# The old value rows of a sliding-window cache: copied inside device memory instead of stored from on-chip tiles

## The chip, the core and the metric

The kernel runs on one core of a Trainium2 chip. The metric is the device time of one launch in microseconds; three runs of the kernel before gave 2320.72, 2321.75 and 2324.44 us, a median of 2321.75 us. TensorE (PE) does the matmuls, VectorE (DVE), ScalarE (ACT) and GpSimd (POOL) the rest, and every DMA of this program is issued by one engine, SyncE (SP), in program order. A DMA moves packets on up to 16 DMA engines of the core; one packet here is one contiguous run of bytes.

## The reference

One inference step of a decoder trunk with two layers: a prompt of 512 tokens and 8 samples of one new token each. Each layer is a half-step SwiGLU FFN, a token mixer, and a second half-step FFN. The mixer has a gated DeltaNet group and a sliding-window attention group. For the samples the attention reads a cache of the last 128 keys and values and returns the cache shifted by one token:

```
def _swa_step(q, k, v, k_buf, v_buf, sinks):
    kk = jnp.concatenate([k_buf, k], axis=1)      # 128 old rows, 1 new row
    vv = jnp.concatenate([v_buf, v], axis=1)
    ...                                           # softmax with a sink, o = p @ vv
    return o, kk[:, T:], vv[:, T:]                # T = 1: drops the oldest row
```

So rows 0 to 126 of the new value cache are rows 1 to 127 of the old one, unchanged, and row 127 is the new token's value. Eight samples, 127 rows of 128 float32 (2 heads of 64): 1016 rows of 512 bytes for each layer.

## The kernel before

All activations stay on chip with features on partitions. Weights are streamed: blocks of 512 KB go into three `raw` buffers, ACT rounds each half block to a float32r head (`whi`), DVE computes the rest (`wlo`), and PE multiplies in three passes. Eight split half blocks can be held. A load of `raw` waits until DVE has given out the `wlo` of the buffer's block before.

The order of all instructions is fixed when the program is built: `Fill` (L96) puts steps of the smaller computations between those of the big products, by an estimate of time (`Clock`, L40). On the chip each engine works in order, so an instruction that waits holds up all behind it on its engine.

The change touches the mixer, `mix` (L748). Its parts, as far as they are needed here:

- The input projection streams 22 tiles of `in_win`. Its small loads are issued first: `wraw`, then the rotary tables `cos` and `sin`, and after the first four tiles the convolution state (`misc<-in_convst`). In layer 0 this begins at about 455 us of the profile, in layer 1 at about 1597 us.
- `swa_sample` (L1330) is the attention of the samples. It loads the old keys into two tiles `kc` and the old values into two tiles `vc`, four samples each, with the cache row on the partition for `vc`. Later it stores the shifted keys (`out_ks<-kc`, L1359), the 127 old value rows of each half (`out_vs<-vc`, L1360), and last the new row (`out_vs<-vrow`). The tiles `vc` also feed the product with the softmax.
- The DeltaNet group builds for each head a matrix `B` on DVE. `dn_inverse` (L930) takes two heads at once: the diagonal blocks of 16 of `B` go out to device memory (`bs<-B`) and come back with another layout (`bb<-bs`); then a long chain of small DVE instructions (`t<-w,bb`, `w<-t`) builds the inverses.
- `swa_block` (L1249) is the attention of the prompt; its scores are the PE products `aux<-swa,swa`, and DVE reads them (`mx`) before PE may write the next ones.

In the program order of SP, the four stores of `swa_sample` and the new row stand directly ahead of `bs<-B`, `bb<-bs`, `bs<-B`, `bb<-bs` of the first two heads, and these ahead of the next three weight loads. Each DMA also uses one of eight completion semaphores in turn, so it waits for the DMA eight places before it to have landed.

Of the kernel before, what the change touches and what calls it, by code (L numbers as in the profile page):

```python
# [23 lines left out]
# Tiles of the input projection: q, k, v of the delta rule by head (c), k, v, q of attention (s), gates (z).  # L24
# [13 lines left out]
class Clock:  # L38
    """An estimate of when the engines are done with what they were given and when tiles are there,
    for the order of the trace."""  # L40
# [41 lines left out]
    def ring(self, tag, n, tile):  # L82
        """A new tile in a ring of n buffers: it is there when the one before it is given up."""
        r = self.rings.setdefault(tag, [])
        r.append(tile)
        if len(r) > n:
            k = self.key(r.pop(0))
            self.rd[self.key(tile)] = max(self.rd.get(k, 0.0), self.wr.get(k, (0.0,))[0])


class Fill:
    """Generators whose steps are put between those of the main products. A step is given to the
    engines when what it waits for should be there; those of a lower rank go first. A generator yields the
    tiles that its next step reads, a condition, or nothing: all that it has done so far."""
# [33 lines left out]
    def step(self):  # L128
        """One step that holds the tensor engine, with others that do not."""
        c = self.clk  # L130
        t = c.pe
        for n in range(TUNE["steps"]):
            e = None
            if all(c.free[q] <= c.pe + v for q, v in BACKLOG.items()):
                e = next((e for e in self.q if e[0] <= c.pe + 0.05 and (e[2] is None or e[2]())), None)
            if e is None:
                return n > 0
            self.run(e)
            if c.pe > t:
                break  # L140
        return True
# [17 lines left out]
class Stream:  # L159
    """Weight blocks in the order in which they are used: loads run ahead, and each half block  # L160
    (four k-tiles) is split into a float32r head and a float32r rest."""
# [10 lines left out]
    def add(self, ap, keep=None):  # L172
        """keep: takes the place of the rings; the split is held back until it says so."""
        self.descs.append(ap)
        n = ap.shape[1]
        for o in range(0, n, 512):
            self.subs.append((len(self.descs) - 1, o, min(512, n - o), o + 512 >= n, keep))

    def advance(self, done, must=-1):
        """Loads and splits as far as the buffers reach and the loads have come, and up to half block  # L180
        must; done: half blocks that are used up."""
        clk = self.ops.clk
        while True:
# [9 lines left out]
            j = len(self.todo)  # L193
# [19 lines left out]
    def rest(self):  # L213
        """The rest of a split is given out after the head of the next one."""
        if self.late:
            j, d, lo, raw, hi = self.late
            self.late = None
            self.ops.tt(out=lo, in0=raw, in1=hi, op=ALU.subtract)
            if d is not None:
                del self.raw[d]  # L220
                self.free_raw = d + 1
# [5 lines left out]
    def take(self, held=0):  # L227
        """The next half block; held: how many before it are still in use."""
        j = self.out
        self.advance(j - held, j)  # L230
        assert j < len(self.todo), (j, len(self.todo), held)
        if self.late and self.late[0] == j:
            self.rest()
            self.advance(j - held)
        self.out += 1
        return self.todo[j]


class Ops:
    """The engines' instructions, counted on the clock."""  # L240
# [96 lines left out]
def trunk(ctx, tc, xT, cT, cst, rope, vec, gu1, dn1, win, wba, wout, gu2, dn2, ada,  # L337
# [16 lines left out]
    # slots in use, and those promised to a part that takes them as it goes  # L354
# [17 lines left out]
    def hold(n):  # L372
        """Waits for n slots; they are given back with a negative number."""
        yield lambda: room_for(n)
        given[0] += n
# [23 lines left out]
    # ---------------------------------------------------------------- adaLN  # L399
# [8 lines left out]
    def ada_mm(t, pa, u=0, first=True, last=True):  # L408
        """m of 512 features, for all sequences, in rows 16 u + sequence: four k-tiles at once in columns
        of the array, summed over them when it is turned to features on partitions."""  # L410
        for k in range(KD):
            r = k % 4
            mm(pa[32 * r:32 * r + 32], lhsT=sc[:, u, k, :], rhs=t[k], start=first and k < 4, stop=last and k >= 4, frac=0.27)
# [6 lines left out]
    def ada_turn(l, g, m_sb, pt=None, n=1):  # L420
        """The n groups from g on to features on partitions, with what is added and multiplied."""
# [12 lines left out]
    def ada_gen(l0):  # L434
        """Works off what is left of adaLN up to layer l0, while there is room for its weights."""
# [29 lines left out]
    # ---------------------------------------------------------------- norm  # L465
    class Norm:
        """RMSNorm, shift and scale of x, half by half, split into head and rest."""
# [11 lines left out]
        def square(self, k, a, end=False):  # L479
            """x of tile k is there: its square joins the sum when the next one comes, or at the end."""  # L480
# [58 lines left out]
    # ---------------------------------------------------------------- products  # L539
    def mmk(out, w, k, src, kk, a, first, last, M=128):  # L540
        """One k-tile of a product in three passes: head by head, head by rest, rest by head."""
        wh, wl = w
        for wi, (wt_, part) in enumerate(((wh, 0), (wh, 1), (wl, 0))):
            mm(out, lhsT=wt_[:, k * M:(k + 1) * M], rhs=src(a, part, kk), start=first and wi == 0, stop=last and wi == 2)
# [11 lines left out]
    def product(src, nk=KD, k0=0, M=128):  # L556
        """One tile of a product, both halves; yields after each k-tile, then the banks."""
# [21 lines left out]
    def head(norm):  # L579
        """The first four tiles of a product, half by half, while the norm of x ends. The blocks  # L580
        hold two tiles by four k-tiles."""
# [24 lines left out]
    def first_head(norm, ada_late):  # L606
        """The head of the first product, by pairs of k-tiles as their shift and scale come, for as many
        of its tiles as there are banks."""
# [35 lines left out]
    def tail(l, j, items, nk, norm, src, last, wait=None):  # L644
        """The last tiles of a product, for one half of the tokens at a time; x and its norm follow.
        items: half, tile, whether its weights come now, whether they are used later, whether they
        are in the rings."""
# [35 lines left out]
    # ---------------------------------------------------------------- FFN  # L683
# [45 lines left out]
    # ---------------------------------------------------------------- mix  # L729
# [18 lines left out]
    def mix(l, norm):  # L748
# [23 lines left out]
        # ------------------------------------------------ gates  # L772
# [57 lines left out]
        # ------------------------------------------------ delta rule: before the scan  # L830
# [99 lines left out]
        def dn_inverse(pr):  # L930
            """Inverses of the blocks of 16 on the diagonal, of two heads."""
# [31 lines left out]
        def dn_merge(h):  # L963
            """Joined to blocks of 32, 64, 128."""
# [32 lines left out]
        # ------------------------------------------------ delta rule: the scan, two heads at a time  # L997
# [3 lines left out]
        def normed(o, zin, dst_hi, dst_lo, key):  # L1001
            """Gated RMSNorm of o (heads on the middle axis), split."""
# [77 lines left out]
        # ------------------------------------------------ delta rule: one step of the samples  # L1080
# [28 lines left out]
        def sample_pair(pr, qv, beg, d8, i8, bc, on):  # L1109
            """Rows 32 j + s of two heads: the products with the state, then what follows from them."""  # L1110
# [89 lines left out]
        # ------------------------------------------------ attention  # L1200
# [129 lines left out]
        def swa_sample():  # L1330
# [26 lines left out]
            for i in range(2):  # L1357
                ops.copy(out=kct[i][:, :, 128], in_=qn[:, 0, 4 * i:4 * i + 4])
                dma(out=ks_o[l, :, 4 * i:4 * i + 4, :], in_=kct[i][:, :, 1:129])  # L1359
                dma(out=vs_o[l, 4 * i:4 * i + 4, 0:127, :].rearrange("s k d -> k s d"), in_=vct[i][1:128])  # L1360
# [56 lines left out]
        # ------------------------------------------------ input projection  # L1417
        rope_t = [slot("cos", F32, (128, T)), slot("sin", F32, (128, T))]
        wraw = slot("wraw", F32, (128, KD, 32))
        dma(out=wraw, in_=wba[l])  # L1420
        dma(out=rope_t[0], in_=rope[:, 0])
# [40 lines left out]
        # b, a: between the others  # L1462
# [26 lines left out]
        # ------------------------------------------------ output projection  # L1489
# [24 lines left out]
    # ---------------------------------------------------------------- order of the weights  # L1514
# [27 lines left out]
    # ---------------------------------------------------------------- run  # L1542
    with tc.manual_schedule():
# [6 lines left out]
        def load(q, j):  # L1550
            """The weights for shift or scale of two k-tiles of x."""
# [105 lines left out]
def layout(i):  # L1657
    """The inputs as the chip takes them: blocks of weights with k on partitions, activations and
    states with features on partitions."""
# [26 lines left out]
    def head4(b):  # L1686
        """The first four tiles as blocks of two tiles by four k-tiles."""
# [77 lines left out]
```

## Time and profile before

| | |
|---|---|
| median of three runs | 2321.75 us (2320.72 to 2324.44) |
| span of the profiled execution | 2320.7 us; no other time is recorded for it |
| mean granted TensorE clock | 0.985 |
| PE busy | 2234.2 us, 96% of the span |
| DVE busy | 1084.8 us, 47% |
| ACT busy | 866.1 us, 37% |
| DMA queue of SP | 172708 packets, 285 MB, 38.4% of 16 engines |

The share of PE is an average: nearly all of the span it is the engine that sets the pace, with a few stretches in which it idles. Such stretches are where work on another engine, or a transfer, can move the end. The granted clock is given as a share of full speed, 2.4 GHz; 0.50 is the lower level of 1.2 GHz.

### The profile page before, as it was taken

The page shows a single profiled execution, that of the slowest core. Times are in us where ns is not written, and L with a number is a line of the kernel's source. Part 1 is how long each engine was busy: PE and PEld are TensorE (multiplying, and loading weights), DVE is VectorE, ACT ScalarE, POOL GpSimd, SP SyncE. Part 2 cuts the span into 40 slices and gives each one's busy share as a digit, 9 for nine tenths or more (in the row PEclk, how much of TensorE's full clock was granted, in tenths as well). Part 3 has the DMA queues.
Part 4 walks back from the last instruction along what each step waited for, and adds up shares of the span by engine and source line. Part 5 has one row for each costly group of instructions (what it writes and reads, how often), then busy time and mean ns, then how long its engine had stood idle before and what let it go on. Part 6 is the DMA issues. An engine that isn't in the chain of part 4 may idle for free.

```text
span 2320.7 us, 43783 instructions
## 1 busy us (share of the span) xinstructions
PE 2234.2 (96%) x18154; PEld 2122.6 (91%) x18154; DVE 1084.8 (47%) x2586; ACT 866.1 (37%) x1861; POOL 76.5 (3%) x73
## 2 busy tenths in 40 slices
PE   7999999999888999999999999999979889999999
PEld 5879999999777988999999999999878779999999
DVE  5323333565788733333344333335667777333332
ACT  4222332355645432233234333224637445333321
POOL 0000000000121000000000000000001200000000
PEclk8999999999899999999999999999989999999999
DMA  8994223343214589422323222324322243222331
GB/s 269 323 329 136 92 85 92 101 77 94 88 50 136 180 314 339 155 92 85 95 86 101 92 91 89 93 83 91 102 81 70 63 146 110 92 92 91 92 109 56
DMA packets 172907, 287.75 MB, mean 124 GB/s; under 512 B 49925, under 2 KB 87461, under 8 KB 172709
## 3 DMA queue, kind: packets, MB, share of 16 engines
q1 hardware_dynamic: 172708, 284.96, 38.4%
q8 instruction: 142, 2.33, 0.4%
q14 instruction: 57, 0.46, 0.1%
HBM read 270.51 MB, written 14.41 MB: 123 GB/s over the span
## 4 chain that ended last, share of the span: by engine, by line
PE 82%; DVE 7%; issue 5%; ACT 3%; DMA 2%; SPq 0%; POOL 0%; DVEq 0%; POOLq 0%
PE acc L263 67%; PE aux L263 15%; DVE wlo L298 1%; DVE s L298 1%; PE aux L273 1%; DMA bs<-B 1%; DVE t L298 1%; ACT sq L290 1%; DVE w L298 1%; DVE hl L298 0%; SPq L258 0%; DVE vr L298 0%; DMA bb<-bs 0%; DMA ada<-in_ada 0%; POOL swa L307 0%
## 5 line engine op out<-in xcount | busy, mean ns | idle before, releaser
L263 PE MATMUL acc<-hh,whi 128*128 128x256 f32 x3440 | 743.9, 290 | 26.9 <-DVE x L298 12.2
L263 PE MATMUL acc<-hh,wlo 128*128 128x256 f32 x3440 | 722.8, 285 | 1.2 <-DVE wlo L298 1.2
L263 PE MATMUL acc<-hl,whi 128*128 128x256 f32 x3440 | 722.9, 285 | 0.0
L290 ACT ACTIVATE whi<-raw 128x512 fp32r<-128x512 f32 (+1 forms) x672 | 406.2, 617 | 785.7 <-PE acc L263 619.7
L298 DVE TENSOR_TENSOR wlo<-raw,whi 128x512 fp32r<-128x512 f32 (+1 forms) x672 | 437.3, 681 | 377.4 <-ACT whi L290 376.9
L263 PEld LDWEIGHTS acc<-hh,whi 128*128 128x128 f32 x3440 | 549.1, 189 | 66.9 <-issue 33.3
L263 PEld LDWEIGHTS acc<-hh,wlo 128*128 128x128 f32 x3440 | 547.4, 189 | 2.5 <-DVE wlo L298 2.5
L263 PEld LDWEIGHTS acc<-hl,whi 128*128 128x128 f32 x3440 | 548.5, 190 | 0.2
L263 PE MATMUL acc<-ghi,whi 128*128 128x256 f32 x1232 | 262.2, 283 | 0.0
L263 PE MATMUL acc<-glo,whi 128*128 128x256 f32 x1232 | 262.2, 283 | 0.0
L263 PE MATMUL acc<-ghi,wlo 128*128 128x256 f32 x1232 | 262.1, 283 | 0.0
L298 DVE TENSOR_TENSOR g<-g,acc 128x256 f32<-128x256 f32 (+1 forms) x168 | 64.2, 422 | 342.5 <-PE acc L263 306.1
L263 PEld LDWEIGHTS acc<-glo,whi 128*128 128x128 f32 x1232 | 197.1, 189 | 0.0
L263 PEld LDWEIGHTS acc<-ghi,wlo 128*128 128x128 f32 x1232 | 196.9, 188 | 0.0
L263 PEld LDWEIGHTS acc<-ghi,whi 128*128 128x128 f32 x1232 | 196.7, 188 | 0.0
L290 ACT ACTIVATE ghi<-g 128x520 fp32r<-128x520 f32 x88 | 56.2, 639 | 219.5 <-DVE g L298 219.5
L298 DVE SCALAR_TENSOR_TENSOR x<-acc,mt,x 128x256 f32<-128x256 f32 x72 | 33.6, 481 | 141.9 <-PE acc L263 141.9
L298 DVE TENSOR_TENSOR glo<-g,ghi 128x520 fp32r<-128x520 f32 x88 | 61.7, 701 | 62.2 <-ACT ghi L290 62.2
L263 PE MATMUL aux<-hl,whi 128*128 128x264 f32 x304 | 86.8, 286 | 0.8 <-DVE hl L298 0.8
L263 PE MATMUL aux<-hh,whi 128*128 128x264 f32 x304 | 87.1, 286 | 0.0
L263 PE MATMUL aux<-hh,wlo 128*128 128x264 f32 x304 | 86.6, 285 | 0.0
L263 PE MATMUL aux<-ada,sc 128*32 128x512 f32 (+1 forms) x640 | 70.9, 571 | 6.7 <-DMA ada<-in_ada 6.7
(289 smaller groups left out, 2149.4 us busy)
## 6 DMA issues: line engine op xcount, KB each, us to landing
raw<-in_gu SPq DMA_DIRECT2D x176, 512.0 KB, 3.3
ada<-in_ada SPq DMA_DIRECT2D x288, 256.0 KB, 5.4
raw<-in_dn SPq DMA_DIRECT2D x64, 512.0 KB, 3.5
raw<-in_win SPq DMA_DIRECT2D x44, 512.0 KB, 3.3
raw<-in_dn SPq DMA_DIRECT2D x32, 384.0 KB, 3.2
raw<-in_wout SPq DMA_DIRECT2D x22, 512.0 KB, 4.0
s<-in_s SPq DMA_DIRECT2D x16, 256.0 KB, 3.9
bv<-vnd SPq DMA_DIRECT2D x16, 256.0 KB, 4.1
```

What stands on the lines that cost most here:

```text
L263: self.nc.tensor.matmul(out, lhsT=lhsT, rhs=rhs, start=start, stop=stop)
L273: self.nc.tensor.transpose(out, in_, ident)
L290: self.nc.scalar.activation(**k)
L298: getattr(self.nc.vector, f)(**k)
```

## The change

In `swa_sample` the two stores of the 127 old value rows go. In their place one DMA of each layer, issued in the input projection between `wraw` and `cos`, copies the rows of all eight samples from the input in device memory to the output in device memory. The tiles `vc` are still loaded, for the product.

```diff
             for i in range(2):
                 ops.copy(out=kct[i][:, :, 128], in_=qn[:, 0, 4 * i:4 * i + 4])
                 dma(out=ks_o[l, :, 4 * i:4 * i + 4, :], in_=kct[i][:, :, 1:129])
-                dma(out=vs_o[l, 4 * i:4 * i + 4, 0:127, :].rearrange("s k d -> k s d"), in_=vct[i][1:128])
...
         wraw = slot("wraw", F32, (128, KD, 32))
         dma(out=wraw, in_=wba[l])
+        dma(out=vs_o[l, :, 0:127, :], in_=vc[l, 1:128].rearrange("k s d -> s k d"))
         dma(out=rope_t[0], in_=rope[:, 0])
         dma(out=rope_t[1], in_=rope[:, 1])
```

The rest of the diff removes comments. On PE, DVE, ACT and POOL the order of the instructions is the same in both kernels; only running numbers in some names differ. On SP it differs in two places of each layer. The first is the start of the input projection of layer 0, on SP (`in_win` are its weights, `in_vc` the old values in device memory):

```order
@@ -52,4 +52,5 @@
 L258 DMA raw<-in_win 128x1024 x6
 L258 DMA wraw<-in_wba 128x256
+L258 DMA out_vs<-in_vc 8x127x128
 L258 DMA cos<-in_rope 128x512
 L258 DMA sin<-in_rope 128x512
```

One transfer is added, with 8 as its outermost size and 127 rows of 128 elements for each sample; two table loads and the weight loads come behind it. The second place is in `swa_sample` of layer 0, again on SP (`out_ks` and `out_vs` are outputs in device memory, `vrow` the new value row, `bs_91` the scratch for `B`):

```order
@@ -69,8 +70,5 @@
 L258 DMA vc<-in_vc 128x512
 L258 DMA raw<-in_win 128x1024
-L258 DMA out_ks<-kc 128x4x128
-L258 DMA out_vs<-vc 127x4x128
-L258 DMA out_ks<-kc 128x4x128
-L258 DMA out_vs<-vc 127x4x128
+L258 DMA out_ks<-kc 128x4x128 x2
 L258 DMA out_vs<-vrow 8x128
 L258 DMA bs_91<-B 128x4x128
```

The two transfers with 127 as the outermost size are gone; the stores of the keys, the new row and `bs<-B` now follow one another.

## Rows read from the trace of the kernel before

**Rows 1.** The page: span and instructions.
```profile
span 2320.7 us, 43783 instructions
```

**Rows 2.** Timeline of PE, layers 0 and 1: start, us, what [idle <-releaser].
```profile
585.96 0.81 PE L263 MATMUL acc<-hh,whi 128*128 128x256 f32 x2 [3.82 <-ACT misc L290]
594.43 2.28 PE L263 MATMUL aux<-swa,swa 64*128 64x256 f32 x8 [6.80 <-DVE mx L298]
...
1728.15 0.62 PE L263 MATMUL acc<-hh,whi 128*128 128x256 f32 x2 [4.13 <-ACT misc L290]
1737.92 2.28 PE L263 MATMUL aux<-swa,swa 64*128 64x256 f32 x8 [8.29 <-DVE mx L298]
```

**Rows 3.** Busy time by stretch, layer 0; then granted clock, DMA share, GB/s.
```profile
560.00:582.00 22.00, 22.00 (x184) 21.07 (x182) 9.16 (x16) 5.11 (x12) 1.69 (x1) 1.00 0.21 56
582.00:595.00 13.00, 2.38 (x12) 1.94 (x10) 11.78 (x44) 4.90 (x12) 0.00 (x0) 0.61 0.25 84
600.00:640.00 40.00, 39.95 (x308) 36.65 (x307) 26.70 (x85) 33.35 (x87) 6.25 (x5) 1.00 0.27 74
```

**Rows 4.** Timeline of ACT and DVE ahead of the first stall.
```profile
584.66 0.63 ACT L290 ACTIVATE whi<-raw 128x512 fp32r<-128x512 f32 x1 [13.62 <-DMA raw<-in_win]
...
557.15 1.11 DVE L298 SCALAR_TENSOR_TENSOR B<-aux,be,dd 128x128 f32<-128x128 f32 x4
582.29 0.29 DVE L298 TENSOR_SCALAR bb<-bb 64x256 f32<-64x256 f32 x1 [11.48 <-DMA bb<-bs]
1725.77 0.28 DVE L298 TENSOR_SCALAR bb<-bb 64x256 f32<-64x256 f32 x1 [13.09 <-DMA bb<-bs]
```

**Rows 5.** Timeline of SP's DMA queue, layers 0 and 1.
```profile
549.00 0.36 SPq L258 DMA_DIRECT2D out_vs<-vc  x1
549.49 11.22 SPq L258 DMA_DIRECT2D out_ks<-kc  x1
560.75 0.97 SPq L258 DMA_DIRECT2D out_vs<-vc  x1
561.77 11.76 SPq L258 DMA_DIRECT2D out_vs<-vrow  x1
573.57 0.39 SPq L258 DMA_DIRECT2D bs<-B  x1
...
1691.30 11.31 SPq L258 DMA_DIRECT2D out_ks<-kc  x1
1703.45 11.94 SPq L258 DMA_DIRECT2D out_vs<-vrow  x1
```

**Rows 6.** SP's DMA queue, 552 to 560 us: packets, MB, share of 16 engines.
```profile
q1 hardware_dynamic: 340, 0.17, 7.2%
```

**Rows 7.** Chain that ended last, in order of time: start, us, what.
```profile
573.57 3.83 DMA bs<-B
577.83 2.22 DMA bs<-B
580.07 2.20 DMA bb<-bs
596.72 1.60 PE acc L263 x6
598.31 1.20 PE aux L263 x8
622.28 0.72 PE acc L263 x6
```

**Rows 8.** Timeline of SP and ACT where the new transfer goes, layer 0.
```profile
455.34 0.42 SPq L258 DMA_DIRECT2D cos<-in_rope  x1
459.95 11.75 SPq L258 DMA_DIRECT2D raw<-in_win  x2
...
479.08 2.18 ACT L290 ACTIVATE whi<-raw 128x512 fp32r<-128x512 f32 x4
```

**Rows 9.** The page, DMA issues: KB each, median us from issue to landing.
```profile
raw<-in_win SPq DMA_DIRECT2D x44, 512.0 KB, 3.3
```

## The prediction

> **What bounds the kernel now.** I read the profile from the end backwards: first the span and the chain that ended last, then PE's timeline for the places where it idles, then the timelines of the engines that end those waits, and last SP's queue and the packets of the stretch.
>
> The profiled execution spans 2320.7 us [rows 1], and no other time is recorded for it; the median of the three runs, 2321.75 us, is 1.05 us more. PE sets the pace almost everywhere, so what counts is where PE waits. One such place lies in each layer's mixer. In layer 0 PE waits 3.82 us for ACT and, six matmuls later, 6.80 us for DVE; in layer 1 it is 4.13 and 8.29 us [rows 2]. Between 582 and 595 us PE works 2.38 of 13 us, and the granted clock of the stretch is 0.61, against 1.00 before and after; DVE works 11.78 us of it [rows 3]. So PE loses twice: it idles, and what follows runs at the lower of its two levels, 1.2 GHz, for a while.
>
> Why are ACT and DVE late there? ACT had waited 13.62 us for a weight block, DVE 11.48 us (layer 0) and 13.09 us (layer 1) for `bb`, the first two heads' blocks coming back from device memory [rows 4]. `B` of the second head was done on DVE at 557.15 + 1.11 = 558.26 us [rows 4], but SP issued the first `bs<-B` at 573.57 us, because two issues ahead of it took 11.22 us (the second `out_ks`) and 11.76 us (`vrow`) [rows 5]. An issue usually takes 0.4 us. Each of the two slow ones stands directly behind an `out_vs<-vc`. Once `bs` was out, it took 3.83 us to land, the second 2.22 and `bb` 2.20 us [rows 7]: the round trip is short, its start is late.
>
> What fills SP's wait is seen in the packets. From 552 to 560 us, when only the first old-value store is moving, the queue has 340 packets and its packet time is 7.2% of 16 engines [rows 6]. One engine of sixteen would be 6.25% and two 12.5%; so the store runs on one engine (records of neighbouring packets overlap a little). 8 us over 340 packets is 23.5 ns each; 127 rows of four samples are 508 packets, 11.9 us, which is the length of each blocked issue.
>
> The Trainium skill has the rule for this in "DMA: Bandwidth & Descriptors", section "Why a DMA increments its semaphore by 16 and not by 1": a DMA from SP takes the largest number up to 16 that divides the outermost sizes of both sides, so 127 partitions go to one engine. The trace agrees, with its 7.2%. The same rule speaks partly against the new transfer, whose outermost size is 8: eight engines, not sixteen.
>
> **What goes.** In each layer two stores of 508 packets on one engine. Then the second `out_ks` and `vrow` are issued by about 551 us, and `bs<-B` goes out as soon as `B` is there: the second head's at about 558.7 us. With 2.2 to 3.8 us for it and 2.2 us for its `bb` [rows 7] the blocks are back at about 565 us. DVE's order is unchanged; it reaches `bb` at 582.29 - 11.48 = 570.81 us, so it no longer waits, with some 6 us to spare. The next weight load stands right behind the second `bb`, so goes out at about 564 us and takes 3.3 us [rows 9]; ACT wants it at 584.66 - 13.62 = 571.04 us and has some 3 us to spare.
>
> PE's first wait, for ACT, then goes whole, since it hung on that weight block. Its second hangs on DVE, whose whole chain moves up by 11.48 us: what released PE at 594.43 us comes at 582.95. PE, running through, is there at 585.96 - 3.82 + 0.72 = 582.86 us (0.72 us is six matmuls at full clock [rows 7]). In layer 1 it is 1737.92 - 13.09 = 1724.83 against 1728.15 - 4.13 + 0.72 = 1724.74 us. A wait of 0.1 us is left, and as DVE is nearly full there I allow 0.4 us a layer for it and the next read of the same kind; DVE has room only later (26.70 of 40 us from 600 on [rows 3]), and there PE is never idle, so the gain is not given back to DVE.
>
> - Idle time of PE: 3.82 + 6.80 + 4.13 + 8.29 = 23.04 us.
> - Clock: six matmuls took 1.60 us behind the stall and 0.72 us at full clock, and the eight `aux` ones 2.28 us against 1.20 for the next eight [rows 2, 7]. Two groups of six and one of eight ran slow in each layer: 2 x 0.88 + 1.08 = 2.84, for two layers 5.68 us.
> - Waits left over: -0.8 us.
>
> Together 27.9 us.
>
> **What comes.** One transfer a layer of 1016 packets, issued at about 455.3 us, ahead of `cos` [rows 8]. The trace has no copy from device memory to device memory, so its time is bounded: from below by eight engines with 127 packets at the 23.5 ns of the stores, 3.0 us; from above by all 1016 packets on one engine, 23.9 us; and twice that if each packet costs double because both ends are in device memory. I take 3.0 us, because the nearest row has packets of the same size and the order shows 8 as the outermost size.
>
> What is queued behind it on SP: `cos`, `sin`, then two weight loads, of which the first is issued at 459.95 us [rows 8]. If the next issue is blocked for the whole transfer, as behind the old stores, `cos` goes out at about 458.8 us and the weight load is still on time. Nobody needs that load soon: it lands at about 463.3 us, and ACT splits it at 479.08 us [rows 8]. So the cover is some 16 us, and the cost of a 3 us transfer is nothing. It has no bounds below nothing either: it releases no one. If the cover were gone, each further microsecond would hold up ACT, and PE behind it. The completion semaphore of the transfer is wanted again eight DMAs later, behind both of those weight loads, so it holds up nothing sooner than they do.
>
> **Sum.** 2320.7 - 27.9 = 2292.8 us for the profiled execution; with the 1.05 us between it and the median, 2293.9, so 2294 us. What is late next is the same pair, DVE's read of the scores against PE, now 0.1 us apart.
>
> **Rivals.**
>
> *The new transfer runs on one engine.* For it: both removed stores did. Against it: 127 is not its outermost size. 455.8 + 23.9 = 479.7 us; the weight load behind it goes out then and lands at 483.4, 4.3 us after ACT wants it. With half of the clock's price above (1.4 us) that is 5.7 us a layer, 11.4 in all: 2305 us.
>
> *The inverse chain is still late.* For it: `bs` and `bb` are two round trips in a row through device memory, just behind 1024 packets of `out_ks`. Against it: 6 us to spare. If `bb` came at 575 us instead of 565, PE would idle some 4 us and pay the 2.84 us for the clock again: 6.9 a layer, 13.7 in all: 2308 us.
>
> *The change doesn't free SP*, because the key stores, with as many rows, block it. For it: one blocked issue is an `out_ks`. Against it: the other is `vrow`, and the blocked time is that of one-engine packets. Then nothing moves: 2322 us.
>
> *Slower.* The new transfer runs on one engine and each packet costs double: 47.8 us, to 503.6; the weight load lands at 507.3, 28.2 us late, plus 2.84 for the clock, minus the 13.95 gained: 17.1 us a layer lost, 2356 us. It decides from the point where the loss equals the gain: a load 11.1 us late, so a transfer of 30.7 us, which is 30 ns a packet on one engine or 242 ns on each of eight. For it: nothing in the trace shows such a copy. Against it: two departures from the rows are needed together.
>
> **How the numbers follow.** The forecast has 0.74, one engine 0.08, the late chain 0.09, nothing freed 0.04, slower 0.05. The forecast's own range is 2291 (none of the allowances needed, a little more regained) to 2300 us (the clock's part not regained: 2298.7). The range for 8 in 10 takes in the two cases of a smaller gain: 2288 to 2308 us. Faster by over 0.2% (4.6 us, about what a measurement of this kernel can tell from no change) is the first three, 0.91; within 0.2% 0.04; slower 0.05.
>
> **What would show it.** In the profile after: no issue of SP over 1 us in `swa_sample`; both `bs<-B` issued by about 559 us; no wait of DVE for `bb` of the first two heads; PE busy through 582 to 595 us at a granted clock of 1.00, and the same in layer 1; the added transfer some 3 us long, and ACT's split at 479 us unmoved. I am wrong if PE idles around 480 us of layer 0, if `bb` is still waited for, or if another stretch of PE's idle time grows by what this one loses.

## The result and the profile after

The changed kernel takes 2292.61 us (median of 4 runs, 2291.18 to 2294.32), the kernel before 2322.31 us (4 runs, 2320.72 to 2324.44). The ratio is 0.9871, 95% interval 0.9857 to 0.9885. The forecast was 2294 us in a range of 2288 to 2308.

The page of the profiled execution, which spans 28.2 us less than before [rows 1]:

```profile
span 2292.5 us, 43781 instructions
PE 2230.0 (97%) x18154; PEld 2118.9 (92%) x18154; DVE 1084.5 (47%) x2586; ACT 866.2 (38%) x1861; POOL 76.5 (3%) x73
```

PE is busy 4.2 us less than before (2234.2) with the same instructions, and idle 62.5 us in place of 86.5. So the gain is 24.0 us of waits and 4.2 us of PE's busy time: the matmuls behind the stalls now run at the higher clock.

SP's DMA queue, layer 0 (start, us, what), at the new transfer's place and in `swa_sample`; it answers to [rows 5] and [rows 8]:

```profile
455.98 0.87 SPq L258 DMA_DIRECT2D out_vs<-in_vc  x1
456.90 1.58 SPq L258 DMA_DIRECT2D cos<-in_rope  x1
458.53 1.17 SPq L258 DMA_DIRECT2D sin<-in_rope  x1
...
549.06 0.94 SPq L258 DMA_DIRECT2D out_ks<-kc  x2
550.12 0.37 SPq L258 DMA_DIRECT2D out_vs<-vrow  x1
553.80 0.38 SPq L258 DMA_DIRECT2D bs<-B  x1
556.40 0.34 SPq L258 DMA_DIRECT2D bb<-bs  x1
558.85 0.36 SPq L258 DMA_DIRECT2D bs<-B  x1
561.06 0.33 SPq L258 DMA_DIRECT2D bb<-bs  x1
561.49 21.68 SPq L258 DMA_DIRECT2D raw<-in_win  x3
```

The two issues of 11.22 and 11.76 us are gone. The first `bs<-B` goes out at 553.80 in place of 573.57 us, and all four small transfers are issued by 561.06. The first weight load behind them follows at 561.49 (the 21.68 us on that row are three issues; ahead of the later two SP waits 15.4 and 5.3 us for DVE).

Timelines of DVE, PE and ACT; they answer to [rows 2, 4, 8]. A row without brackets had no idle time before it:

```profile
571.29 0.28 DVE L298 TENSOR_SCALAR bb<-bb 64x256 f32<-64x256 f32 x1
583.55 1.29 PE L263 MATMUL aux<-swa,swa 64*128 64x256 f32 x8
479.62 2.18 ACT L290 ACTIVATE whi<-raw 128x512 fp32r<-128x512 f32 x4
```

DVE finds `bb` there, 11.00 us earlier than before. PE starts the eight products 10.88 us earlier, without a wait, and they take 1.29 us instead of 2.28. ACT's split at the new transfer's place has no wait. It comes 0.54 us later, and so does all of this execution by then: the weight load just ahead of the stores of `swa_sample` goes out at 546.57 in place of 546.02 us.

Busy time by stretch (length, then PE, PEld, DVE, ACT, POOL, then granted clock, DMA share, GB/s), against [rows 3], and two stretches of layer 1:

```profile
560.00:582.00 22.00, 22.00 (x182) 21.12 (x180) 18.85 (x49) 8.54 (x20) 1.70 (x1) 1.00 0.19 60
582.00:595.00 13.00, 13.00 (x104) 11.94 (x104) 12.72 (x51) 4.76 (x18) 0.00 (x0) 1.00 0.25 81
600.00:640.00 40.00, 39.79 (x293) 34.01 (x292) 28.43 (x80) 32.70 (x68) 8.02 (x6) 1.00 0.29 85
1717.00:1729.00 12.00, 12.00 (x102) 12.00 (x101) 11.58 (x44) 7.83 (x34) 1.03 (x1) 1.00 0.11 15
1729.00:1742.00 13.00, 13.00 (x103) 12.28 (x103) 6.07 (x15) 12.94 (x32) 2.59 (x2) 1.00 0.47 143
```

From 582 to 595 us PE works all 13 us at a clock of 1.00, where it had worked 2.38 at 0.61. DVE, which worked 9.16 of 22 us ahead of the stall, now works 18.85: its chain of small instructions has moved there.

### The profile page after: what moved, and what is told of

Read it like the earlier page. It is cut to its first block, busy times and chain, and to the rows that moved or that the text cites. A ratio compares the mean times of both kernels' runs of the same rounds, so it can differ in the third digit from the quotient of the medians.

```text
span 2292.5 us, 43781 instructions
## 1 busy us (share of the span) xinstructions
PE 2230.0 (97%) x18154; PEld 2118.9 (92%) x18154; DVE 1084.5 (47%) x2586; ACT 866.2 (38%) x1861; POOL 76.5 (3%) x73
## 4 chain that ended last, share of the span: by engine, by line
PE 85%; DVE 6%; issue 5%; ACT 3%; DMA 1%; POOL 0%; SPq 0%; DVEq 0%; POOLq 0%
PE acc L263 68%; PE aux L263 15%; DVE wlo L298 1%; DVE s L298 1%; PE aux L273 1%; ACT sq L290 1%; DVE hl L298 0%; DVE t L298 0%; DVE vr L298 0%; DVE w L298 0%; ACT whi L290 0%; POOL swa L307 0%; DVE ss L298 0%; DVE sq L298 0%; DVE x L298 0%
```

## The experiments

Each time stands beside runs of the kernel before on the same chip (medians 2322.3 to 2323.7 us). Edits are against the kernel after, unless said otherwise; `out` is `vs_o[l, :, 0:127, :]` and `src` is `vc[l, 1:128]`.

**1. The new transfer left out.** The old value rows 0 to 126 of the output are not written at all.

```diff
-        dma(out=out, in_=src.rearrange("k s d -> s k d"))
```

> The changed kernel without its new transfer: rows 0 to 126 of the value cache are not written at all. If the new transfer is hidden, as forecast, the time is that of the changed kernel, 2292.6 us, within 1 us, and the stretches around 456 and 582 us look the same. If the transfer costs something where it stands (a blocked SP, a late weight block), this kernel is faster than the changed one by that cost: up to 4 us a layer, so down to 2285 us.

Measured: 2293.86 us (2292.91 to 2294.26), ratio 0.9875 [0.9860, 0.9889]. The whole gain is there without the copy, and none that stands clear of noise is added by leaving it out: the copy costs nothing that can be measured, and the gain comes from what was taken out of `swa_sample`.

**2. The same copy with 127 outermost, in the new place.**

```diff
-        dma(out=out, in_=src.rearrange("k s d -> s k d"))
+        dma(out=out.rearrange("s k d -> k s d"), in_=src)
```

> The same new transfer, in the same place, with 127 as the outermost size in place of 8. Theory: it runs on one engine, 1016 packets at 23.5 ns, 23.9 us; the issue of cos behind it takes some 23 us, the weight load behind that goes out at about 480 us and lands 4 us after ACT wants it: 5.7 us a layer lost against the changed kernel, 2304 us. Rival: the number of engines doesn't matter this far from any use, PE never idles around 480 us, 2293 us.

Measured: 2312.75 us (2309.62 to 2314.28), ratio 0.9955 [0.9940, 0.9970]. SP's queue, ACT's and PE's timeline, layer 0, then two stretches as above, and SP's packets from 458 to 478 us (packets, MB, share of 16 engines):

```profile
454.49 0.84 SPq L258 DMA_DIRECT2D out_vs<-in_vc  x1
455.37 23.54 SPq L258 DMA_DIRECT2D cos<-in_rope  x1
478.96 0.49 SPq L258 DMA_DIRECT2D sin<-in_rope  x1
479.57 0.83 SPq L258 DMA_DIRECT2D raw<-in_win  x2
...
485.67 1.15 ACT L290 ACTIVATE whi<-raw 128x512 fp32r<-128x512 f32 x2 [7.45 <-DMA raw<-in_win]
488.74 2.07 PE L263 MATMUL aux<-sq,cs 128*128 128x512 f32 x2 [7.00 <-ACT sq L290]
```

```profile
485.00:490.00 5.00, 1.26 (x3) 0.73 (x3) 3.54 (x6) 3.86 (x7) 0.00 (x0) 0.50 1.55 74
490.00:495.00 5.00, 5.00 (x14) 2.76 (x12) 1.63 (x4) 3.86 (x8) 0.00 (x0) 0.55 1.04 187
```

```profile
q1 hardware_dynamic: 841, 0.43, 7.1%
```

The mechanism of this rival is what the prediction said: the share of 7.1% is that of one engine, as in [rows 6], the issue behind the transfer is held 23.54 us, the weight load goes out at 479.57 (forecast 479.7), and ACT and then PE wait. The price is not: PE idles 7.00 us in layer 0 and 6.29 in layer 1 (forecast 4.3), and the granted clock from 485 to 495 us is 0.50 and 0.55. The load landed some 6 us after its issue, not 3.3. `cos`, `sin` and two weight loads now go out within 2 us, and the DMA share from the load's issue to its landing (479.5 to 485.7 us) is 0.82; that this traffic is the reason was not tested by itself.

**3. The two old stores, in their old place, cut by rows.** Against the kernel before; every store keeps its source, its queue and its bytes.

```diff
-                dma(out=vs_o[l, 4 * i:4 * i + 4, 0:127, :].rearrange("s k d -> k s d"), in_=vct[i][1:128])
+                for k0, k1 in ((0, 112), (112, 127)):
+                    dma(out=vs_o[l, 4 * i:4 * i + 4, k0:k1, :].rearrange("s k d -> k s d"), in_=vct[i][k0 + 1:k1 + 1])
```

> The kernel before, with each of its two stores from on-chip tiles cut in 112 and 15 partitions, in the old place. Theory (the one engine of a 127-partition transfer blocks SP): the parts run on 16 and 15 engines, no issue of SP is over 2 us, and the time is that of the changed kernel, 2293 us, though rows come from on-chip tiles and two DMAs a layer are added. Rival (the gain comes from taking the rows from device memory, or from having fewer DMAs ahead of bs): it stays at 2322 us or goes above.

Measured: 2296.17 us (2293.30 to 2296.78), ratio 0.9883 [0.9868, 0.9898]. SP's queue:

```profile
548.30 1.09 SPq L258 DMA_DIRECT2D out_vs<-vc  x2
549.50 0.69 SPq L258 DMA_DIRECT2D out_ks<-kc  x1
550.23 1.71 SPq L258 DMA_DIRECT2D out_vs<-vc  x2
...
552.68 0.39 SPq L258 DMA_DIRECT2D bs<-B  x1
```

Four stores in place of two, and no issue is held. So neither the on-chip source nor the number of DMAs nor their place made the stall, but that 127 rows went to one engine. The time is 3.6 us above the kernel after; as the two intervals overlap, that is not clear of noise.

**4. The copy with 8 outermost, in the old place between the key stores.**

```diff
                 dma(out=ks_o[l, :, 4 * i:4 * i + 4, :], in_=kct[i][:, :, 1:129])
+                if i == 0:
+                    dma(out=out, in_=src.rearrange("k s d -> s k d"))
...
-        dma(out=out, in_=src.rearrange("k s d -> s k d"))
```

> The new transfer with 8 as the outermost size, but issued where the old stores were, between the two stores of the keys. Theory: eight engines, 127 packets each, some 3 to 4 us; the next issue is blocked for 2 to 3 us, until about 553 us, and bs of the second head goes out at 559 us as in the changed kernel: 2293 us. Rival (the gain comes from moving the transfer out of the stores' place): 2300 us or more, bs late by what the transfer takes.

Measured: 2294.80 us (2294.03 to 2296.32), ratio 0.9882 [0.9865, 0.9898]. The second key store, issued behind the copy, is held about a microsecond longer (549.65, 1.54 us in SP's queue), and no engine waits for it. The place 90 us earlier gave nothing that can be measured.

**5. Two copies with 127 outermost in the new place**, the second into a scratch tensor in device memory.

```diff
-        dma(out=out, in_=src.rearrange("k s d -> s k d"))
+        dma(out=out.rearrange("s k d -> k s d"), in_=src)
+        vx = dr.tile([NS, 128, 128], F32, name=f"vx{l}", tag=f"vx{l}")
+        dma(out=vx[:, 0:127, :].rearrange("s k d -> k s d"), in_=src)
```

> In the changed kernel's place, the 127-outermost transfer twice (the second goes to a scratch in device memory that nobody reads). Theory: 2032 packets on one engine, 47.8 us, until about 504 us; the weight load behind lands 28 us after ACT wants it, PE idles that long and runs at the lower clock level for a while: 31 us a layer above the changed kernel, 2354 us, slower than the kernel before. Rival: PE has split blocks in hand and idles clearly less, under 2325 us.

Measured: 2359.04 us (2356.29 to 2359.62), ratio 1.0149 [1.0132, 1.0166]. SP's queue and ACT:

```profile
456.15 23.56 SPq L258 DMA_DIRECT2D vx<-in_vc  x1
479.76 23.80 SPq L258 DMA_DIRECT2D cos<-in_rope  x1
...
510.61 2.44 ACT L290 ACTIVATE whi<-raw 128x512 fp32r<-128x512 f32 x4 [31.51 <-DMA raw<-in_win]
```

Each of the transfers holds the issue behind it. This is the prediction's slower case, made by two transfers rather than by dearer packets, at close to the price that it gave (2356). ACT waits 31.51 us for the load, forecast 28.2.

**6. The copy with 127 outermost in the old place, on ACT's queue.** The transfer stays on one engine, but SP no longer stands behind it.

```diff
                 dma(out=ks_o[l, :, 4 * i:4 * i + 4, :], in_=kct[i][:, :, 1:129])
+                if i == 0:
+                    nc.scalar.dma_start(out=out.rearrange("s k d -> k s d"), in_=src)
...
-        dma(out=out, in_=src.rearrange("k s d -> s k d"))
```

> The 127-outermost transfer (1016 packets on one engine, about 24 us) in the old stores' place, but issued by ACT, so that SP's own issues are not behind it. Theory (SP's blocked issue is the cost): bs and bb go out on time, their few packets on the busy engine pass between those of the transfer, and the time is that of the changed kernel, 2293 us, at most 2 us more. Rival (the occupied DMA engine itself is the cost: everything that needs its packets lands late, whoever issued it): bs and bb land after some 575 us, DVE waits for bb again, and the time is 2315 us or more.

Measured: 2309.15 us (2307.01 to 2309.90), ratio 0.9936 [0.9921, 0.9951], between the two expectations. SP's queue and PE's timeline, then the wait of SP for this copy (us in total, times, longest):

```profile
552.40 0.38 SPq L258 DMA_DIRECT2D bs<-B  x1
558.34 0.35 SPq L258 DMA_DIRECT2D bb<-bs  x1
559.11 0.36 SPq L258 DMA_DIRECT2D bs<-B  x1
572.98 0.33 SPq L258 DMA_DIRECT2D bb<-bs  x1
...
587.14 2.28 PE L263 MATMUL aux<-swa,swa 64*128 64x256 f32 x8 [4.94 <-DVE mx L298]
```

```profile
SPq L258 <- DMA out_vs<-in_vc: 7.6, 1, 7.6
```

No issue is held, and yet the second `bb` goes out only at 572.98. Two things delay it. Each `bs` takes about 6 us to land. And SP waits 7.6 us more for the copy itself, although `bb` needs nothing of it: in the trace both carry the same one of the eight completion semaphores, and the copy's last packet ends at 572.63, just ahead of that `bb`. The run alone does not say how much of the time is the shared engine's and how much is that semaphore's, so two more were made.

**7. The same on GpSimd's queue**, whose completion counts on a semaphore that no DMA of SP uses.

```diff
-                    nc.scalar.dma_start(out=out.rearrange("s k d -> k s d"), in_=src)
+                    nc.gpsimd.dma_start(out=out.rearrange("s k d -> k s d"), in_=src)
```

> The copy with 127 outermost, 1016 packets on one engine, in the old place, issued by GpSimd: its completion counts on a semaphore of its own, so that no DMA of SP waits for it, which spoiled the run on ACT's queue. Theory (what cost 28 us is that SP's next issue is held for 11 to 12 us behind each one-engine store): SP isn't held, the first bs lands some 3 us later than after the change, as on ACT's queue (5.9 in place of 2.6 us), the second bs at about 565, and its bb, issued then, lands by 571, about when DVE reaches it (571.29): 2293 to 2297 us, no stall of PE over 1 us between 582 and 595. Rival (a busy engine is enough, since 127 or 128 row transfers use that engine too): each of the four round trips of bs and bb waits for it, bb is over 5 us late and PE stalls by as much in each layer: 2305 us or more. Had the run on ACT's queue lost its 16.5 us to the engine and not to the semaphore, this one would come to 2309 again.

Measured: 2325.17 us (2322.26 to 2329.39, 10 runs), ratio 1.0012 [1.0002, 1.0021]: all of the gain gone. The time lies where the alternative put it (2305 us or more), but not quite by its way: of the two `bs` and two `bb` only the first `bs` was long out. GpSimd, DVE and SP's queue, layer 0, and then DVE's two copies in the kernel after:

```profile
547.35 6.83 POOL L1361 DMA_DIRECT2D out_vs<-in_vc  x1
548.15 6.00 DVE L298 COPY kc<-qn 128x4 f32<-128x4 f32 x2
584.36 0.28 DVE L298 TENSOR_SCALAR bb<-bb 64x256 f32<-64x256 f32 x1 [7.96 <-DMA bb<-bs]
...
558.84 0.38 SPq L258 DMA_DIRECT2D bs<-B  x1
578.97 0.35 SPq L258 DMA_DIRECT2D bb<-bs  x1
```

```profile
548.86 0.24 DVE L298 COPY kc<-qn 128x4 f32<-128x4 f32 x2
```

The run brought two things of its own. While GpSimd worked on its issue, 6.83 us, DVE's two copies took 6.00 us in place of 0.24, and both key stores went out only behind them. And SP waited 19.7 us for the first `bs`: the packet records show this queue's copy as 127 packets of 4096 B (173 ns each) and 1905 of 32 B, and from 572 to 578 us about five of the 4096 B ones in each microsecond with about five of SP's 512 B ones between them. It shows that a copy on another queue can take all of the gain; it does not answer the question of experiment 6.

**8. On ACT's queue again, a few instructions later**, so that an `xs` transfer at about 595 us is the next to use the copy's semaphore.

```diff
-                if i == 0:
-                    nc.scalar.dma_start(out=out.rearrange("s k d -> k s d"), in_=src)
...
             yield qp, kct[0], kct[1]
+            nc.scalar.dma_start(out=out.rearrange("s k d -> k s d"), in_=src)
```

> The copy with 127 outermost on ACT's queue once more, issued a few instructions later (after the row of new values, about 551), so that the DMA that takes its completion semaphore next is an xs transfer at about 595 and no longer bb of the second head. SP is held neither at an issue nor for the copy; the copy's 1016 packets still sit on one engine from about 552 to 576, under both bs and both bb. If the one engine, shared with SP's queue in turns, costs only the 3 us per bs seen on ACT's queue (5.9 in place of 2.6 us), the second bb is issued at about 566 and lands by 570, before DVE reaches it: 2293 to 2297 us, no stall of PE over 1 us between 582 and 595; then it was the semaphore that made the run on ACT's queue 16.5 us longer. If the shared engine is enough by itself, bb is late again by 5 us or more, PE stalls in each layer, and the time is 2305 us or more, as with GpSimd's queue, where bs waited 19.7 us.

Measured: 2297.74 us (2295.35 to 2299.59), ratio 0.9898 [0.9882, 0.9915]. SP's queue, PE in layer 0, and then packets, MB and share of 16 engines by queue from 555 to 560 us (q1 is SP's, q10 ACT's):

```profile
553.21 0.38 SPq L258 DMA_DIRECT2D bs<-B  x1
559.61 0.35 SPq L258 DMA_DIRECT2D bb<-bs  x1
560.40 0.41 SPq L258 DMA_DIRECT2D bs<-B  x1
566.63 0.33 SPq L258 DMA_DIRECT2D bb<-bs  x1
567.06 16.88 SPq L258 DMA_DIRECT2D raw<-in_win  x3
...
584.27 1.34 PE L263 MATMUL aux<-swa,swa 64*128 64x256 f32 x8 [1.26 <-DVE mx L298]
```

```profile
q10 hardware_dynamic: 180, 0.09, 6.1%
q1 hardware_dynamic: 55, 0.02, 1.6%
```

The copy is still on one engine, from 552 to 580 us, beside both `bs` and both `bb`, and SP no longer waits for it. Yet the second `bb` goes out at 566.63, and PE waits 1.26 us in each layer where it waited 3.82 and 6.80 [rows 2] or, with the semaphore, some 5. So the 11.4 us between experiments 6 and 8 are the semaphore's, and what cost the kernel before its time was that SP's other transfers stood behind the one-engine stores in SP's own queue. Sharing the engine seems to cost something too: this run is 5.1 us above the kernel after, just beyond the expected 2293 to 2297, with intervals that barely overlap, and the wait of 1.26 us is above the 1 us that was expected at most.

## Why the prediction was right

- *One-engine stores hold SP.* Right: gone without them, gone when the same stores are cut to 112 and 15 rows (3), back at 23.54 us for 1016 packets on one engine (2), which is the 23.9 us worked out from 23.5 ns a packet. Whether the issue itself is held or its packets queue behind the others on that engine was not separated; another queue removes both.
- *`bs` and `bb` on time.* The second `bs` was forecast at about 558.7 us and issued at 558.85; the next weight load at 564 and issued at 561.49. DVE was to reach `bb` at 570.81; it did at 571.29, in an execution 0.54 us later there.
- *PE's waits and clock.* Waits 23.04 less 0.8 us forecast, 24.0 measured over the whole span; the clock's part 5.68 forecast, 4.2 measured as PE's busy time. The sum is 27.9 against 28.2. That it is so close is in part luck: the waits came out 1.8 us above their term and the clock's part 1.5 below its own. The two waits in each layer went whole, 23.04 us; the other 1.0 us of waits is spread in small pieces over the span and belongs to no step of the forecast. The allowance of 0.8 us for left-over waits was not needed: from 582 to 595 us there is none. The margin there is thin, as forecast: in experiment 8 the same read of DVE holds PE 1.26 us.
- *The new transfer.* Forecast 3.0 us with the next issue held as long, hidden. It ran 4.1 us in layer 0 and 3.5 in layer 1. Its packets' records are 27 ns long, as those of the old stores are; the 23.5 ns of the forecast is what passes from one packet to the next on one engine. From 459 to 460 us the queue moves this copy alone, `q1 hardware_dynamic: 327, 0.17, 55.2%` (packets, MB, share of 16 engines); with 7.2% for one engine [rows 6] that is about eight. The issues behind it were held less than it ran, 1.58 and 1.17 us in layer 0, 2.28 and 0.43 in layer 1. Hidden it is (1).
- *The rivals.* The one-engine transfer was put at 2305 us and measured 2312.75 (2): the term that failed is the landing of the weight load, 3.3 us, the median of the kernel before [rows 9]; here it took some 6. The mechanism, the blocked time and the clock's part (2.8 us forecast; PE is busy 2.6 us longer than in the kernel after) were right. The slower case was put at 2356 and measured 2359.04 (5), with the same term short by some 3 us. That the key stores hold SP, or that the round trips stay late, is out.
- *The forecast's own range.* Its upper end, 2298.7 us without the clock's part, leaves out the allowance of 0.8 us as well; with it, it is 2299.5. Nothing rests on it.

The Trainium skill ("DMA: Bandwidth & Descriptors", section "Why a DMA increments its semaphore by 16 and not by 1") has the rule that stands behind the choice of 3.0 us over 23.9, and experiments 2 and 4 show it for a copy inside device memory: the same bytes with 8 outermost hold the next issue 1.54 us, with 127 outermost 23.54.

## What to carry to other kernels

When several small issues in a row take over 10 us each, look at the DMA ahead of them: one whose outermost size is 127, as here, runs on one engine, and everything behind it in that queue is late by its whole length, though DMA as a whole is at 7%. Turn its order or cut it, so that more engines share it (8 outermost, or 112 and 15 rows, here); source, place and count then mattered little. Moving such a transfer to another queue was the weaker remedy here: it keeps the engine busy for as long, and its completion semaphore may be waited for by a DMA that has nothing to do with it (6).

## What was not expected of the hardware

- A one-engine copy on one queue slows the DMAs of another, though it takes one engine of sixteen. In experiment 8 from 555 to 560 us ACT's copy moved 180 packets while SP's queue, with `bs` still out, got 55; `bs` took 6.3 us to land (median from issue), against 2.4 in the kernel after, and a weight load 6.4 against 3.4. The Trainium skill ("DMA: Bandwidth & Descriptors", section "Queues, rings and completion order") says that an engine goes round the queues that have work for it and drains a packet of one, there a group of descriptors, before it switches. From 558 to 559 us the two queues moved 22 and 21 packets, which fits turns, but from 556 to 558 us 79 and 6; how long a turn is, this run does not show.
- A DMA issued by GpSimd held DVE: its copies took 6.00 us in place of 0.24 beside an issue of 6.83 us. Only that one run shows it, and it doesn't show by what.
- A copy inside device memory was no dearer than a store from on-chip tiles: the record of a 512 B packet is 27 ns long in both, and on one engine 841 packets of the copy took 20 us (2), 23.8 ns each, against 23.5 ns for the store [rows 6].
- The completion semaphores, used in turn, cost 11.4 us in experiment 6 between DMAs of two different queues that share no data.
